# Convolution units that end behind the next eviction, and a light piece behind each convolution piece, in a hybrid decoder trunk

## The chip, the cores and the metric

The kernel runs on one core of one Trainium2 chip. The metric is the time of one execution on the device in microseconds. The core's engines that matter here are PE (TensorE, matrix products), ACT (ScalarE, activations), DVE (VectorE, elementwise work and reductions), POOL (GpSimd) and SP (SyncE, which here only issues loads).

## The reference

Two pre-norm residual layers (`DEPTH` 2) over 256 tokens of width 1024, in float32. Each layer projects the normalised stream once and feeds three causal token mixers side by side; their outputs are projected, gated, merged, projected again and added to the stream. A final RMSNorm closes the trunk. Cut to what matters:

```python
h = rms_norm(x, norm_w[layer])
proj = jnp.einsum('bsd,de->bse', h, w_in[layer])          # 12832 columns
(a_xbc, a_z, a_dt, b_q, b_k, b_v, b_z,
 c_q, c_k, c_v, c_f, c_z, gates) = jnp.split(proj, split_at, axis=-1)
y_a = mamba2_branch(a_xbc, a_z, a_dt, ...)       # convolution of width 4, SiLU, SSD scan, gate, group norm
y_b = sliding_window_branch(b_q, b_k, b_v, b_z, ...)      # rope, window 128, sinks, gate
y_c = forgetting_attention_branch(c_q, c_k, c_v, c_f, c_z, ...)   # decay bias from c_f, gate
branch = jnp.einsum('bsiw,iwd->bsid', jnp.stack([y_a, y_b, y_c], axis=2), w_proj[layer])
g = jax.nn.sigmoid(gates.reshape(b, s, 3, d) + gate_bias[layer])
x = x + jnp.einsum('bsd,de->bse', jnp.sum(g * branch, axis=2), w_out[layer])
```

In the Mamba-2 branch the 2048 columns `a_xbc` (1024 of x, 512 of B, 512 of C) pass a causal depthwise convolution, `silu(sum_j w[j] * u[t-3+j] + bias)`, before the scan.

## The kernel before

**Products.** Every product of activations and weights is made of three float32r products: a value is split into a high part (`hi`) and the remainder (`lo`), and hi x hi, lo x hi and hi x lo are added up in PSUM. A weight part (1024 columns' worth in each of 128 partitions, 512 KB) is loaded by SP into a `raw` tile (six buffers); ACT copies it to `hi` (L261) and DVE subtracts to get `lo` (L262), six buffers each, with at most four parts split ahead (`AHEAD`).

**Pieces and units.** The weights are cut into pieces, mostly of 256 columns (two parts), some of 272 or 512. A piece is worked off in two units. For a 256-column piece of channels (`chan`, L440) a unit is 128 channels by 256 tokens: 24 matmuls into one of three `mm` buffers of PSUM. For token-major pieces (`tok`, L447) a unit is 128 tokens by the piece's columns. Behind its matmuls each unit evicts its PSUM buffer by ACT or DVE and does its own elementwise work:

- convolution (`u_conv`, L672): ACT copies the buffer (L682) and makes bias plus the last tap (L683); DVE adds the other three taps (L686); ACT takes Tanh (L689); DVE closes the SiLU (L690). There are eight such pieces in a layer, 16 units.
- branch gate (`u_z`, L761): ACT Tanh (L770), then DVE (L773, or L777 and L778 for the Mamba branch), which reads the buffer too.
- values of forgetting attention (`u_cv`, L815), its keys (`u_ck`, L833) and queries (`u_cq`, L843): copies on ACT. Two of the value pieces also carry the logits of the time step and of the forget gate.
- merge gate (`u_gate`, L886): DVE adds the bias (L894), ACT takes Tanh (L895).
- projection of a branch (`u_proj`, L900): DVE multiplies by the gate (L936, L939).

**Order.** The order of PE is written out: the list `ops` holds the units, and the loop at L1061 fills it. Before the loop's main part come values, keys and queries of the sliding-window attention. Then, in this stage (the "convolution stage"), B and C of the scan (four convolution pieces) and x (four), with other pieces between them (`lights`, one list for each layer); the swa gate pieces (`zb`), two value pieces (`cv(512, 0)`, `cv(768, 1)`), the merge gates and projection of branch 1 (`gates_proj(1)`). Behind it follow keys, queries and gates of forgetting attention, then branch 0 and branch 2. ACT, DVE and POOL are ordered by the scheduler of the language, which goes by the order of the program and by its own times of what is ready; each engine then runs its list in order.

**The planner.** The work of attention and scan is not in `ops`. It stands in generators that are launched (`launch`, L103) with a branch number and a due time, and are stepped by `pump` (L130) at the end of each unit, when the planner's own clock (an estimate of PE time, L91) has passed the due time and a condition holds. Four quads of heads of sliding-window attention (`swa_quad`, branch 1) follow one another by one token `pp`; each scan group (`ssd_group`, branch 0) waits until no generator of branch 1 is left (L697) and for the token `ssd`; the four quads of forgetting attention (`fox_quad`, branch 2) take the token `bias`, fetch their bias by DMA, wait `D_BDMA` 4.0, mask it on POOL, wait until their queries are there and `D_BIAS` 2.0 more, and then take `pp`. `drain(br)` (L140) forces what is left of a branch. `split_late` (L958) drains a branch and splits its gated output for the projection; in layer 0 it stands a convolution piece ahead of the projection of branch 1, in layer 1 straight ahead of it (L1093, L1134). `group_norm` (L788) is launched with `D_GN1` 4.0 and goes on `D_GN2` 6.0 later.

**Buffers.** Keys and queries of forgetting attention share the four buffers `qt` with the queries of the swa quads. Convolution units use three of the 14 buffers `L1`.

Of the kernel before, what the change touches and what calls it, by code (L numbers as in the profile page):

```python
# [13 lines left out]
AF = mybir.ActivationFunctionType  # L14
ALU = mybir.AluOpType

P = 128
# [6 lines left out]

D_SOFT, D_SOFT2, D_EVAC, D_SSD, D_SSD2 = 7.0, 3.0, 3.0, 8.0, 3.0
D_K, D_Q, D_QK, D_G0, D_FOX, D_BDMA, D_BIAS = 6.0, 5.5, 2.0, 8.0, 0.0, 4.0, 2.0
D_GN1, D_GN2, D_CUM, D_H, D_M = 4.0, 6.0, 12.0, (4.8, 6.4), 5.0
BUDGET = 1.35
T_PP, T_SSD, T_BIAS = 1, 1, 1
N_RAW, N_SPLIT = 6, 6  # L30
# [14 lines left out]
def hybrid_trunk(  # L45
# [17 lines left out]
    def T(tag, shape, dtype=F32, bufs=None):  # L63
        count[0] += 1
        return sb.tile(shape, dtype, tag=tag, name=f"{tag}_{count[0]}",
                       bufs=bufs if bufs is not None else BUFS.get(tag, 1))
# [184 lines left out]
    def halves(ap):  # L251

        return ap.rearrange("p (a i) -> p a i", a=2)
# [418 lines left out]
    def u_conv(y, u, c):  # L672
        def f(w):
            p = chan(y, w, c)
            if u == 8:
                y.bcT = T("L8", [P, 8, S])
            if u == 0:
                y.xs = T("L8", [P, 8, S])
            dst = y.xs[:, u, :] if u < 8 else y.bcT[:, u - 8, :]
            a = T("L1", [P, S])  # L680
            x_ = T("L1", [P, S])
            act(halves(x_), p, AF.Copy)  # L682
            act(halves(a), p, AF.Identity, scale=y.vec[:, 48 + u:49 + u], bias=y.vec[:, 64 + u:65 + u])  # L683
            for j in (2, 1, 0):
                s = 3 - j
                stt(a[:, s:S], x_[:, 0:S - s], y.vec[:, 16 * j + u:16 * j + u + 1], a[:, s:S],  # L686
                    op0=ALU.mult, op1=ALU.add)
            th = T("L1", [P, S])
            act(th, a, AF.Tanh)  # L689
            stt(dst, th, 1.0, a, op0=ALU.add, op1=ALU.mult)  # L690
            if u < 8 and u % 2 == 1:
                launch(0, ssd_group(y, u // 2), D_G0)
            pump()
        return f

    def ssd_group(y, g):
        yield lambda: not any(m[2] == 1 for m in waiting)  # L697
# [63 lines left out]
    def u_z(y, br, u, c):  # L761
        def f(w):
            p = chan(y, w, c)
            if u == 0 and br != 0:
                y.sz[br] = T("L8", [P, NK, S])
            if u == 0 and br == 0:
                y.yh[br] = T("L8", [P, 2, NK, P], F32R)
                y.yl[br] = T("L8", [P, 2, NK, P], F32R)
            th = T("L1", [P, S])
            act(halves(th), p, AF.Tanh, scale=0.5)  # L770
            y.zdone.add((br, u))
            if br != 0:
                stt(halves(y.sz[br][:, u, :]), halves(th), 1.0, p, op0=ALU.add, op1=ALU.mult)  # L773
            else:
                drain(0)
                sz = T("L1", [P, S])
                stt(halves(sz), halves(th), 1.0, p, op0=ALU.add, op1=ALU.mult)  # L777
                tt(y.xs[:, u, :], y.xs[:, u, :], sz, op=ALU.mult)  # L778
                sq = T("L1", [P, S])
                act(sq, y.xs[:, u, :], AF.Square)  # L780
                y.sq.append(sq)
                if u % 2 == 1:
                    tt(y.sq[-2], y.sq[-2], y.sq[-1], op=ALU.add)
                    launch(3 if u < 4 else 4, group_norm(y, u // 2, y.sq[-2]), D_GN1)
            pump()
        return f
# [28 lines left out]
    def u_cv(y, c, t, i=None):  # L815

        def f(w):
            p = tok(y.hTh, y.hTl, w, t)
            if y.cv is None:
                y.cv = T("L8", [P, 2, D])  # L820
            m = w.n if i is None else w.n - 16
            rn = 1.0 if y.rn is None else y.rn[:, t:t + 1]
            if i is None:
                act(halves(y.cv[:, t, c:c + m]), p, AF.Copy, scale=rn)
            else:
                n = w.n // 2
                act(y.cv[:, t, c:c + n], p[:, 0, :], AF.Copy, scale=rn)
                act(y.cv[:, t, c + n:c + m], p[:, 1, 0:m - n], AF.Copy, scale=rn)
                logits(y, t, i, p[:, 1, m - n:n])
            pump()  # L830
        return f

    def u_ck(y, j, c):  # L833
        def f(w):
            p = chan(y, w, c)
            y.ckT[j] = T("qt", [P, 2, S])
            act(halves(y.ckT[j][:, 0, :]), p, AF.Copy)
            if j % 2 == 0:
                launch(2, fox_quad(y, j), D_FOX)
            pump()  # L840
        return f
# [8 lines left out]
        return f  # L850

    def fox_quad(y, j):
        yield "bias"
        bs = []
        for p in range(2):
            bias = T("bias", [P, 2, 3 * P])
            nc.scalar.dma_start(bias[:, :, P:3 * P],
                                y.cumd[2 * (j + p):2 * (j + p) + 2, 1, :].partition_broadcast(P))
            bs.append(bias)
        yield D_BDMA  # L860
        for bias in bs:
            for dst, src in ((slice(0, P), slice(P, 2 * P)), (slice(2 * P, 3 * P), slice(2 * P, 3 * P))):
                for i in range(2):
                    nc.gpsimd.affine_select(out=bias[:, i, dst], in_=bias[:, i, src],  # L864
                                            compare_op=ALU.is_ge, fill=NEG, base=0,
                                            pattern=[[-1, P]], channel_multiplier=1)
        yield lambda: j + 1 in y.cqdone and clock["t"] >= y.cqdone[j + 1] + D_BIAS
        kqs = [y.ckT[j], y.ckT[j + 1]]

        def products(score):  # L870
            for p, kq in enumerate(kqs):
                for b in range(2):
                    for i in range(2):
                        r = slice(64 * i, 64 * i + 64)
                        mm(score(p, i, b), kq[r, 1, b * P:(b + 1) * P], kq[r, 0, 0:(b + 1) * P],
                           start=True, stop=True)

        def scored():
            tokens["bias"] += 1

        yield from attn_quad(products, lambda p, i, b: bs[p][:, i, P * b:P + 2 * P * b], None, y.cv,
                             lambda p, i: slice(P * (j + p) + 64 * i, P * (j + p) + 64 * i + 64),
                             lambda: y.sz[2][:, j:j + 2, :], lambda: (2, j + 1) in y.zdone, scored)


    def u_gate(y, br, c, t):  # L886

        def f(w):
            if t == 0:
                y.gb = T("L2", [P, 512])  # L890
                nc.scalar.dma_start(y.gb, gate_bias[y.l, br:br + 1, c:c + 512].to_broadcast([P, 512]))
            p = tok(y.hTh, y.hTl, w, t)
            g = T("L2", [P, 512])
            tt(halves(g), p, halves(y.gb), op=ALU.add)  # L894
            act(g, g, AF.Tanh, scale=0.5)  # L895
            y.gate[t] = g
            pump()
        return f
# [162 lines left out]
    for y in layers:  # L1061
# [3 lines left out]
        y.gate, y.qT, y.ckT, y.sz, y.yh, y.yl, y.sq, y.h, y.ss, y.var, y.zdone, y.cqdone = {}, {}, {}, {}, {}, {}, [], {}, {}, {}, set(), {}  # L1065
        y.u = y.cv = None
        y.logits = 0

        def cols(c0, n=256):
            return sub([(0, w[:, c0:c0 + n])], n)  # L1070
# [15 lines left out]
        def gates_proj(br):  # L1086
# [3 lines left out]

            def p(b):
                c = 512 * b
                if b == 0 and br != 0 and (br, l) != (1, 0):  # L1093
                    op(None, lambda y=y: split_late(y, br))
                i = sub([(0, w_proj[l, br, :, c:c + 512])], 512)
                if b == 0 and br == 0:
                    op(i, u_proj2(y, br))
                else:
                    op(i, u_proj(y, br, c, 0), u_proj(y, br, c, 1))
# [24 lines left out]
            op(rcols(C_BQ + 256 * g), *u_bq(y, g))  # L1124
        op(None, lambda y=y: layer_vec(y))
        z1(C_ZB, 1, 0)

        cv(512, 0)
        cv(768, 1)
        heavy = [(C_B + 256 * b, 8 + 2 * b) for b in range(4)] + [(C_XS + 256 * b, 2 * b) for b in range(4)]  # L1130
        gp = gates_proj(1)
        zb = [lambda b=b: z1(C_ZB, 1, b) for b in (1, 2, 3)]
        if l == 0:
            lights = {0: [zb[0]], 1: [zb[1]], 3: [zb[2]], 5: [gp.pop(0)], 6: [lambda: op(None, lambda y=y: split_late(y, 1))], 7: [gp.pop(0)]}  # L1134
        else:
            lights = {0: [zb[0]], 2: [zb[1]], 3: [zb[2]], 4: [gp.pop(0)], 6: [gp.pop(0)]}
        for i, (c0, u) in enumerate(heavy):
            op(cols(c0), u_conv(y, u, 0), u_conv(y, u + 1, P))
            for light in lights.get(i, ()):
                light()  # L1140
        for f in gp:
            f()

        for b, zb in enumerate(((), (0,), (1,), (2, 3))):
            op(cols(C_CK + 256 * b), u_ck(y, 2 * b, 0), u_ck(y, 2 * b + 1, P))
            op(cols(C_CQ + 256 * b), u_cq(y, 2 * b, 0), u_cq(y, 2 * b + 1, P))
            for z in zb:
                z1(C_ZC, 2, z)
        for f in gates_proj(0):
# [213 lines left out]
```

## Time and profile before

| | |
|---|---|
| median of 3 runs | 845.81 us (844.84 to 847.25) |
| profiled execution | 846.9 us |
| its span, first to last instruction | 845.2 us |
| PE busy | 828.2 us, 98% |
| DVE busy | 652.4 us, 77% |
| ACT busy | 507.1 us, 60% |
| mean granted clock of PE | 0.996 |

Times in the rows are microseconds from the span's start, and mean times of one instruction are nanoseconds. A row of the timeline gives start, length, engine, line, operation, tiles and shapes; in square brackets stands how long the engine had been idle before it and what it waited for. `hi`, `lo`, `raw`, `mm` (PSUM of the pieces) and `mx` (PSUM of everything else) are tiles; `L` stands for the general SBUF buffers. PE's busy time is modelled, and it is no measure of how full the array is: two matmuls overlap in it.

### The profile page before, as it was taken

The numbers are of one execution on the slowest core, as the hardware profiler recorded it, in microseconds if no ns is written. First come the engines' busy times: TensorE is split into PE (matmuls) and PEld (weight loads), VectorE is DVE, ScalarE is ACT, GpSimd is POOL, SyncE is SP. The second block draws the span as 40 slices with busy tenths as digits, with TensorE's granted clock in tenths as the row PEclk, the third lists the DMA queues.
The fourth block names the chain that finished last, engine by engine and source line by source line (L and its number), as shares of the span: only waits on it lengthen the run. The fifth ranks groups of instructions, "written<-read, shape, count | busy, mean of one in ns | idle before, by whom it ended". The sixth has DMA issues, their size and how long they took to land.

```text
span 845.2 us, 16836 instructions
## 1 busy us (share of the span) xinstructions
PE 828.2 (98%) x6341; PEld 766.2 (91%) x6341; DVE 652.4 (77%) x1418; ACT 507.1 (60%) x1030; POOL 94.2 (11%) x149
## 2 busy tenths in 40 slices
PE   8999999999999999999999999998999999999996
PEld 7999988889999998888999999887899999988896
DVE  6978798898786778665778797988877767785665
ACT  7747667656666666353664676765556666654442
POOL 3330000000111011110005100000001110111000
PEclk9999999999999999999999999999999999999999
DMA  9967554577646556675687556645765565576632
GB/s 302 272 177 223 158 150 146 186 237 202 201 141 180 151 164 215 197 248 177 219 271 207 177 169 214 185 139 187 218 184 163 162 175 151 162 236 212 212 100 75
DMA packets 129563, 159.46 MB, mean 189 GB/s; under 512 B 7970, under 2 KB 98202, under 8 KB 129482
## 3 DMA queue, kind: packets, MB, share of 16 engines
q1 hardware_dynamic: 114960, 140.53, 55.1%
q10 hardware_dynamic: 13690, 16.24, 6.2%
q0 software_dynamic: 832, 1.62, 0.7%
q8 instruction: 50, 0.82, 0.4%
q14 instruction: 31, 0.25, 0.1%
HBM read 154.63 MB, written 2.16 MB: 186 GB/s over the span
## 4 chain that ended last, share of the span: by engine, by line
PE 72%; DVE 14%; ACT 6%; issue 3%; DMA 3%; POOL 0%; SPq 0%; ACTq 0%; POOLq 0%; DVEq 0%
PE mm L97 63%; PE mx L97 6%; DVE lo L262 5%; DVE L L686 3%; PE mx L101 2%; ACT hi L261 2%; DMA L<-cumd 2%; ACT pp L548 2%; DMA L<-in_x_dram 1%; DVE pp L560 1%; DVE L L690 1%; DVE L L262 1%; ACT L L577 1%; DVE pp L542 1%; DVE L L724 1%
## 5 line engine op out<-in xcount | busy, mean ns | idle before, releaser
L262 DVE TENSOR_TENSOR lo<-raw,hi 128x1024 fp32r<-128x1024 f32 (+2 forms) x276 | 315.6, 1159 | 85.1 <-ACT hi L261 78.7
L97 PE MATMUL mm<-L,hi 128*128 128x256 f32 x2112 | 373.2, 278 | 3.3 <-ACT L L683 1.6
L97 PEld LDWEIGHTS mm<-L,hi 128*128 128x128 f32 x2112 | 326.9, 192 | 11.8 <-issue 6.0
L261 ACT ACTIVATE hi<-raw 128x1024 fp32r<-128x1024 f32 (+2 forms) x276 | 266.3, 981 | 104.8 <-PE mm L97 85.5
L97 PE MATMUL mm<-hi,L 128*128 128x512 f32 (+2 forms) x1232 | 325.1, 352 | 3.0 <-DVE L L262 2.7
L97 PE MATMUL mm<-L,lo 128*128 128x256 f32 x1056 | 290.4, 275 | 0.0
L97 PEld LDWEIGHTS mm<-hi,L 128*128 128x128 f32 x1232 | 217.5, 190 | 27.3 <-DVE L L262 3.5
L97 PE MATMUL mm<-lo,L 128*128 128x512 f32 (+2 forms) x616 | 214.2, 349 | 0.0
L97 PEld LDWEIGHTS mm<-L,lo 128*128 128x128 f32 x1056 | 202.6, 192 | 0.1
L97 PEld LDWEIGHTS mm<-lo,L 128*128 128x128 f32 x616 | 116.7, 190 | 11.7
L864 POOL TENSOR_SCALAR_AFFINE_SELECT bias<-bias 128x128 f32<-128x128 f32 x64 | 29.5, 498 | 398.9 <-DMA bias<-cumd 381.5
L548 ACT ACTIVATE pp<-pp,nm 128x128 f32<-128x128 f32 (+1 forms) x128 | 56.6, 443 | 16.3 <-DVE nm L542 16.1
L686 DVE SCALAR_TENSOR_TENSOR L<-L,vec,L 128x255 f32<-128x255 f32 (+2 forms) x96 | 45.9, 478 | 2.0 <-ACT L L683 0.9
L689 ACT ACTIVATE L<-L 128x256 f32<-128x256 f32 x32 | 13.4, 417 | 46.5 <-DVE L L686 46.5
L560 DVE TENSOR_SCALAR pp<-pp,rsum 128x128 f32<-128x128 f32 (+1 forms) x128 | 32.2, 315 | 0.5
L770 ACT ACTIVATE L<-mm 128x256 f32<-128x256 f32 x48 | 17.9, 372 | 22.2 <-PE mm L97 18.1
L895 ACT ACTIVATE L<-L 128x512 f32<-128x512 f32 x24 | 15.1, 628 | 25.8 <-DVE L L894 25.5
L577 ACT ACTIVATE L<-mx 128x512 f32<-128x512 f32 x48 | 27.0, 595 | 1.8 <-PE mx L101 1.4
L101 PE MATMUL mx<-ident,pp 128*128 128x128 f32 x192 | 26.8, 275 | 0.0
L542 DVE CUSTOM_DVE_ANT_0 pp<-mx,wmask,nsink 128x128 f32<-128x128 f32 x64 | 23.9, 411 | 1.4 <-PE mx L97 1.4
L261 ACT ACTIVATE L<-L 128x512 fp32r<-128x512 f32 (+1 forms) x36 | 18.4, 531 | 10.8 <-DVE L L811 7.3
L894 DVE TENSOR_TENSOR L<-mm,L 128x512 f32<-128x512 f32 x24 | 16.4, 684 | 9.9 <-PE mm L97 9.9
(190 smaller groups left out, 719.5 us busy)
## 6 DMA issues: line engine op xcount, KB each, us to landing
raw<-in_w_in_dram SPq DMA_DIRECT2D x191, 512.0 KB, 4.6
raw<-in_w_proj_dram SPq DMA_DIRECT2D x48, 512.0 KB, 4.8
raw<-in_w_out_dram SPq DMA_DIRECT2D x16, 512.0 KB, 4.9
L<-cumd ACTq DMA_DIRECT2D x8, 512.0 KB, 6.2
bias<-cumd ACTq DMA_DIRECT2D x16, 256.0 KB, 4.0
L<-in_gate_bias_dram ACTq DMA_DIRECT2D x12, 256.0 KB, 5.3
raw<-in_w_in_dram SPq DMA_DIRECT2D x4, 408.0 KB, 3.5
raw<-in_w_in_dram SPq DMA_DIRECT2D x4, 384.0 KB, 4.9
```

The costliest lines, as they stand in the source:

```text
L97: nc.tensor.matmul(o, a, b, **kw)
L101: nc.tensor.transpose(o, a, i)
L261: keep(act)(hi, src, AF.Copy)
L262: keep(tt)(lo, src, hi.bitcast(F32), op=ALU.subtract)
L542: nc.vector.tensor_tensor_reduce(out=pp[:, i, sl], in0=score(p, i, b), in1=biases(p, i, b), scale=-0.125, scalar=1.0e30 if ns is None else ...
L548: act(pp[:, i, sl], pp[:, i, sl], AF.Exp, scale=-1.0, bias=nm[:, e:e + 1], accum_out=sums[:, e:e + 1])
L560: ts(pp[:, i, sl], pp[:, i, sl], rs[:, 2 * i + b:2 * i + b + 1], 0.5, op0=ALU.mult, op1=ALU.mult)
L577: act(pT, pt, AF.Copy)
L686: stt(a[:, s:S], x_[:, 0:S - s], y.vec[:, 16 * j + u:16 * j + u + 1], a[:, s:S], op0=ALU.mult, op1=ALU.add)
L770: act(halves(th), p, AF.Tanh, scale=0.5)
L864: nc.gpsimd.affine_select(out=bias[:, i, dst], in_=bias[:, i, src], compare_op=ALU.is_ge, fill=NEG, base=0, pattern=[[-1, P]], channel_mul ...
L894: tt(halves(g), p, halves(y.gb), op=ALU.add)
```

## The change

A convolution unit is cut in two. Its eviction and its three taps stay; Tanh, the closing multiply and the launch of the scan group become a function `end`, which is put on a list. The next unit that calls `finish` behind its own eviction on ACT runs what is on the list, with its ACT instructions queued behind that eviction (`issue_after` fixes the order on ACT, without a wait). Convolution, gate, value, key and merge-gate units call it; queries and projections do not.

The two layers now have one order. Two swa gate pieces come first, and then each of the eight convolution pieces is followed by one other piece: the two value pieces, two swa gate pieces, the first merge gate of branch 1, the first keys and the first queries of forgetting attention, and the first projection of branch 1 with `split_late` straight ahead of it, in both layers. The quads of forgetting attention wait for a flag, `y.fox`, which is set behind the projection of branch 1. `D_GN1` goes from 4.0 to 5.0.

```diff
-D_GN1, D_GN2, D_CUM, D_H, D_M = 4.0, 6.0, 12.0, (4.8, 6.4), 5.0
+D_GN1, D_GN2, D_CUM, D_H, D_M = 5.0, 6.0, 12.0, (4.8, 6.4), 5.0
...
-            act(halves(a), p, AF.Identity, scale=y.vec[:, 48 + u:49 + u], bias=y.vec[:, 64 + u:65 + u])
+            finish(act(halves(a), p, AF.Identity, scale=y.vec[:, 48 + u:49 + u], bias=y.vec[:, 64 + u:65 + u]))
             for j in (2, 1, 0):
                 s = 3 - j
                 stt(a[:, s:S], x_[:, 0:S - s], y.vec[:, 16 * j + u:16 * j + u + 1], a[:, s:S],
                     op0=ALU.mult, op1=ALU.add)
-            th = T("L1", [P, S])
-            act(th, a, AF.Tanh)
-            stt(dst, th, 1.0, a, op0=ALU.add, op1=ALU.mult)
-            if u < 8 and u % 2 == 1:
-                launch(0, ssd_group(y, u // 2), D_G0)
+            def end():
+                th = T("L1", [P, S])
+                act(th, a, AF.Tanh)
+                stt(dst, th, 1.0, a, op0=ALU.add, op1=ALU.mult)
+                if u < 8 and u % 2 == 1:
+                    launch(0, ssd_group(y, u // 2), D_G0)
+            ends_later.append(end)
             pump()
         return f
+    ends_later = []
+    def finish(out):
+        with tc.issue_after(out.ins):
+            while ends_later:
+                ends_later.pop(0)()
...
     def fox_quad(y, j):
+        yield lambda: y.fox
         yield "bias"
...
-                if b == 0 and br != 0 and (br, l) != (1, 0):
+                if b == 0 and br != 0:
                     op(None, lambda y=y: split_late(y, br))
...
         z1(C_ZB, 1, 0)
-        cv(512, 0)
-        cv(768, 1)
+        z1(C_ZB, 1, 1)
         heavy = [(C_B + 256 * b, 8 + 2 * b) for b in range(4)] + [(C_XS + 256 * b, 2 * b) for b in range(4)]
         gp = gates_proj(1)
-        zb = [lambda b=b: z1(C_ZB, 1, b) for b in (1, 2, 3)]
-        if l == 0:
-            lights = {0: [zb[0]], 1: [zb[1]], 3: [zb[2]], 5: [gp.pop(0)], 6: [lambda: op(None, lambda y=y: split_late(y, 1))], 7: [gp.pop(0)]}
-        else:
-            lights = {0: [zb[0]], 2: [zb[1]], 3: [zb[2]], 4: [gp.pop(0)], 6: [gp.pop(0)]}
+        lights = [lambda: cv(512, 0), lambda: cv(768, 1), lambda: z1(C_ZB, 1, 2), lambda: z1(C_ZB, 1, 3),
+                  gp.pop(0), lambda: ck(0), lambda: cq(0), gp.pop(0)]
         for i, (c0, u) in enumerate(heavy):
             op(cols(c0), u_conv(y, u, 0), u_conv(y, u + 1, P))
-            for light in lights.get(i, ()):
-                light()
+            lights[i]()
         for f in gp:
             f()
-        for b, zb in enumerate(((), (0,), (1,), (2, 3))):
-            op(cols(C_CK + 256 * b), u_ck(y, 2 * b, 0), u_ck(y, 2 * b + 1, P))
-            op(cols(C_CQ + 256 * b), u_cq(y, 2 * b, 0), u_cq(y, 2 * b + 1, P))
+        op(None, lambda y=y: setattr(y, "fox", True))
+        for b, zb in ((1, (0,)), (2, (1,)), (3, (2, 3))):
+            ck(b)
+            cq(b)
             for z in zb:
                 z1(C_ZC, 2, z)
```

`ck(b)` and `cq(b)` add the key and the query piece b, as the two removed lines did.

More of the change, by code (lines that the diff above doesn't have):

```diff
@@ L769, in f @@
             th = T("L1", [P, S])
-            act(halves(th), p, AF.Tanh, scale=0.5)
+            finish(act(halves(th), p, AF.Tanh, scale=0.5))
             y.zdone.add((br, u))
@@ L823, in f @@
             if i is None:
-                act(halves(y.cv[:, t, c:c + m]), p, AF.Copy, scale=rn)
+                finish(act(halves(y.cv[:, t, c:c + m]), p, AF.Copy, scale=rn))
             else:
@@ L827, in f @@
                 act(y.cv[:, t, c:c + n], p[:, 0, :], AF.Copy, scale=rn)
-                act(y.cv[:, t, c + n:c + m], p[:, 1, 0:m - n], AF.Copy, scale=rn)
+                finish(act(y.cv[:, t, c + n:c + m], p[:, 1, 0:m - n], AF.Copy, scale=rn))
                 logits(y, t, i, p[:, 1, m - n:n])
@@ L836, in f @@
             y.ckT[j] = T("qt", [P, 2, S])
-            act(halves(y.ckT[j][:, 0, :]), p, AF.Copy)
+            finish(act(halves(y.ckT[j][:, 0, :]), p, AF.Copy))
             if j % 2 == 0:
@@ L894, in f @@
             tt(halves(g), p, halves(y.gb), op=ALU.add)
-            act(g, g, AF.Tanh, scale=0.5)
+            finish(act(g, g, AF.Tanh, scale=0.5))
             y.gate[t] = g
@@ L1067, in hybrid_trunk @@
         y.logits = 0
+        y.fox = False
         def cols(c0, n=256):
@@ L1126, in hybrid_trunk, with ck, cq @@
         z1(C_ZB, 1, 0)
-        cv(512, 0)
-        cv(768, 1)
+        z1(C_ZB, 1, 1)
         heavy = [(C_B + 256 * b, 8 + 2 * b) for b in range(4)] + [(C_XS + 256 * b, 2 * b) for b in range(4)]
         gp = gates_proj(1)
-        zb = [lambda b=b: z1(C_ZB, 1, b) for b in (1, 2, 3)]
-        if l == 0:
-            lights = {0: [zb[0]], 1: [zb[1]], 3: [zb[2]], 5: [gp.pop(0)], 6: [lambda: op(None, lambda y=y: split_late(y, 1))], 7: [gp.pop(0)]}
-        else:
-            lights = {0: [zb[0]], 2: [zb[1]], 3: [zb[2]], 4: [gp.pop(0)], 6: [gp.pop(0)]}
+        def ck(b):
+            op(cols(C_CK + 256 * b), u_ck(y, 2 * b, 0), u_ck(y, 2 * b + 1, P))
+        def cq(b):
+            op(cols(C_CQ + 256 * b), u_cq(y, 2 * b, 0), u_cq(y, 2 * b + 1, P))
+        lights = [lambda: cv(512, 0), lambda: cv(768, 1), lambda: z1(C_ZB, 1, 2), lambda: z1(C_ZB, 1, 3),
+                  gp.pop(0), lambda: ck(0), lambda: cq(0), gp.pop(0)]
         for i, (c0, u) in enumerate(heavy):
             op(cols(c0), u_conv(y, u, 0), u_conv(y, u + 1, P))
-            for light in lights.get(i, ()):
-                light()
+            lights[i]()
         for f in gp:
             f()
-        for b, zb in enumerate(((), (0,), (1,), (2, 3))):
-            op(cols(C_CK + 256 * b), u_ck(y, 2 * b, 0), u_ck(y, 2 * b + 1, P))
-            op(cols(C_CQ + 256 * b), u_cq(y, 2 * b, 0), u_cq(y, 2 * b + 1, P))
+        op(None, lambda y=y: setattr(y, "fox", True))
+        for b, zb in ((1, (0,)), (2, (1,)), (3, (2, 3))):
+            ck(b)
+            cq(b)
             for z in zb:
```

## The prediction, on record before the result was known

> **What bounds the kernel now.** I read the page first, then busy time by stretch, then the PE's own waits, then what stood ahead of the instruction that ended each wait. The page, and the stretches (columns: length, PE, weight loads, DVE, ACT, POOL, clock, DMA share, GB/s):
>
> ```profile
> span 845.2 us, 16836 instructions
> ...
> PE 828.2 (98%) x6341; PEld 766.2 (91%) x6341; DVE 652.4 (77%) x1418; ACT 507.1 (60%) x1030; POOL 94.2 (11%) x149
> ...
> raw<-in_w_in_dram SPq DMA_DIRECT2D x191, 512.0 KB, 4.6
> ```
> ```profile
> 54.00:182.00 128.00, 125.11 (x1080) 115.57 (x1079) 110.14 (x290) 87.75 (x210) 5.97 (x14) 1.00 0.58 176
> 182.00:416.00 234.00, 233.71 (x1661) 214.53 (x1661) 170.17 (x338) 133.40 (x248) 25.18 (x33) 1.00 0.63 192
> 288.00:324.00 36.00, 35.71 (x290) 33.89 (x287) 27.34 (x63) 23.91 (x47) 4.35 (x4) 1.00 0.53 155
> 468.00:585.00 117.00, 113.32 (x977) 104.76 (x977) 99.72 (x271) 80.40 (x199) 5.64 (x14) 0.99 0.57 176
> ```
>
> PE is the bound, and the change neither adds nor removes a matmul. What can be won is what PE loses waiting: 2.9 us in the convolution stage of layer 0 (54 to 182), 3.7 us in that of layer 1 (468 to 585), 0.3 us in the long stretch behind. There DVE is busy for 86% (110.14 of 128), against 73% in the long stretch. These are its larger waits there, by the timeline:
>
> ```profile
> 119.31 0.28 PE L97 MATMUL mm<-L,hi 128*128 128x256 f32 x1
> 121.19 0.38 PE L97 MATMUL mm<-L,hi 128*128 128x256 f32 x1 [1.61 <-ACT L L683]
> ...
> 128.19 0.38 PE L97 MATMUL mm<-L,hi 128*128 128x256 f32 x1 [0.72 <-DVE L L773]
> ...
> 539.70 0.38 PE L97 MATMUL mm<-L,hi 128*128 128x256 f32 x1 [0.51 <-DVE L L773]
> ...
> 563.75 0.35 PE L97 MATMUL mm<-L,hi 128*128 128x256 f32 x1 [0.46 <-DVE L L894]
> ...
> 575.00 0.38 PE L97 MATMUL mm<-lo,L 128*128 128x512 f32 x1
> 575.22 0.38 PE L97 MATMUL mm<-hi,L 128*128 128x512 f32 x1
> 578.31 0.80 PE L97 MATMUL mm<-hi,L 128*128 128x512 f32 x1 [2.71 <-DVE L L262]
> 578.89 0.63 PE L97 MATMUL mm<-lo,L 128*128 128x512 f32 x1
> 579.32 1.06 PE L97 MATMUL mm<-hi,L 128*128 128x512 f32 x2
> 580.17 0.63 PE L97 MATMUL mm<-lo,L 128*128 128x512 f32 x1
> 580.60 1.06 PE L97 MATMUL mm<-hi,L 128*128 128x512 f32 x2
> 581.46 0.47 PE L97 MATMUL mm<-lo,L 128*128 128x512 f32 x1
> 581.76 0.60 PE L97 MATMUL mm<-hi,L 128*128 128x512 f32 x2
> ```
>
> The first four stand where a new unit needs a PSUM buffer (there are three `mm` buffers) that has not been evicted. ACT around the first two, DVE for the second, and ACT for the third:
>
> ```profile
> 119.99 0.42 ACT L689 ACTIVATE L<-L 128x256 f32<-128x256 f32 x1 [1.84 <-DVE L L686]
> 120.32 0.37 ACT L682 ACTIVATE L<-mm 128x256 f32<-128x256 f32 x1
> 120.58 0.56 ACT L683 ACTIVATE L<-mm,vec 128x256 f32<-128x256 f32 x1
> ...
> 126.93 0.42 ACT L689 ACTIVATE L<-L 128x256 f32<-128x256 f32 x1 [2.38 <-DVE L L686]
> ```
> ```profile
> 127.73 0.41 DVE L773 SCALAR_TENSOR_TENSOR L<-L,mm 128x256 f32<-128x256 f32 x1
> ```
> ```profile
> 538.22 0.42 ACT L689 ACTIVATE L<-L 128x256 f32<-128x256 f32 x1 [0.60 <-DVE L L686]
> ```
>
> The Tanh that closes a convolution unit (L689) stands on ACT ahead of the next unit's eviction (L682 and L683 of a convolution, or the Tanh of a gate with DVE's L773 behind it), and waits there for the unit's three multiply-adds on a full DVE. PE's buffer is free only after that.
>
> **The change, part by part.** Durations that I use (columns: count, busy us, mean ns, idle before), and, from the chain of waits, a 256-column piece on PE, two units of 24 matmuls:
>
> ```profile
> L262 DVE TENSOR_TENSOR lo<-raw,hi 128x1024 fp32r<-128x1024 f32 (+2 forms) x276 | 315.6, 1159 | 85.1 <-ACT hi L261 78.7 <-PE mm L97 4.9
> ...
> L686 DVE SCALAR_TENSOR_TENSOR L<-L,vec,L 128x255 f32<-128x255 f32 (+2 forms) x96 | 45.9, 478 | 2.0 <-ACT L L683 0.9
> ...
> L690 DVE SCALAR_TENSOR_TENSOR L<-L,L 128x256 f32<-128x256 f32 x32 | 13.5, 421 | 6.5 <-ACT L L689 6.5
> ...
> L689 ACT ACTIVATE L<-L 128x256 f32<-128x256 f32 x32 | 13.4, 417 | 46.5 <-DVE L L686 46.5
> ```
> ```profile
> 271.38 5.36 PE mm L97 x48
> ```
>
> *Ends behind the next eviction.* 32 Tanh and 32 closing multiplies move; none is added, so their own cost is nil. ACT waits 46.5 us ahead of Tanh in all, but only the waits that reach PE are worth time: the first is 121.19 − 119.31 = 1.88, less the usual 0.11 (5.36/48), so 1.77; that is its idle time plus 0.16, and so the others are 0.88 and 0.67. Sum 3.3 us. Tanh stood idle 1.84, 2.38 and 0.60 us there. With a unit more of grace (2.68 us) all three waits would go, since each is shorter: **−3.3**. The least is 0, if ACT only waits a unit later. Tanh now comes 2.7 us later, or behind a whole 10 us projection piece for the last unit; what reads it, a scan group, is launched from the same place with 8 planner microseconds to spare.
>
> *A light piece behind each convolution piece.* A convolution piece costs DVE 2 × 1.159 + 6 × 0.478 + 2 × 0.421 = 6.0 us, more than PE's 5.36; a key or query piece of forgetting attention costs it only the two splits, 2.3 us. Two convolution pieces in a row (two such pairs ahead of the projection in each layer) put 12.1 us of DVE under 10.7 us of PE; after, none stand together. The moved pieces (two of forgetting attention ahead of the projection; the two value pieces, one swa gate piece and, in layer 0, the merge-gate piece by a few places) bring all their work with them: the same matmuls, splits, evictions and loads on the SP queue, in another order. The load queue keeps six parts ahead, 16 us of PE, against a landing of 4.6 us, so loads cost nothing; without that lead each moved part would cost up to that. DVE's total up to the projection grows by 4.6 us in 10.7 us of PE, so its share stays near 86%, and I keep a small new wait in each layer, priced by the 0.51 row plus 0.16: **+1.3** (from 0 to twice that).
>
> *The projection behind the last convolution piece.* The large wait is for the last part of the gated swa output in `split_late`:
>
> ```profile
> 571.84 0.68 DVE L590 TENSOR_TENSOR L<-mx,L 128x512 f32<-128x512 f32 x1
> ...
> 577.58 0.68 DVE L262 TENSOR_TENSOR L<-L,L 128x512 fp32r<-128x512 f32 x1
> ```
>
> From L590 to the end of that split pass 6.4 us, and PE asked for it at 575.44, 3.6 us after L590 began. The swa quads keep their place in PE's order, while the projection comes two pieces, 10.7 us, later, less the 0.67 of waits gone ahead of it: 13.6 us of room against 6.4. The wait goes: 578.31 − 575.22 − 0.22 = 2.87. Behind it eight matmuls take 581.76 − 578.31 = 3.45 us in place of 8 × 0.22, at half rate: 1.69 more. **−4.6.** Layer 0 loses the convolution piece that stood between its splits and its projection, but has the same room.
> The Trainium skill, TensorE: Matmul & The Clock Gate, section What's actually happening, gives about 3.4 us of idleness as what halves the clock; here 2.71 us were enough, so the trace and the page differ. By the page the 1.69 us would not belong to this wait and the sum would be 1.7 us smaller.
>
> *The merge-gate piece* (two 512-column units) is followed by a convolution piece in layer 1 already, where the 0.46 us wait for L894 stands: splits, not Tanh, are ahead of it. That order now comes in layer 0 too: **+0.6** (0 to 1.2).
>
> *Forgetting attention's gate.* Its first quad no longer starts at its keys but when the flag is set behind the projection, then takes 4.0 planner microseconds, so two units. Rows of the first and last scores, the last quad's DVE work, and, below, what the stage behind leaves free:
>
> ```profile
> 216.53 1.58 PE L97 MATMUL mx<-qt 64*128 64x128 f32 x16
> ...
> 282.68 1.58 PE L97 MATMUL mx<-qt 64*128 64x128 f32 x16
> ```
> ```profile
> 283.75 0.29 DVE L542 CUSTOM_DVE_ANT_0 pp<-mx,bias 128x128 f32<-128x128 f32 x1
> ...
> 287.94 1.01 DVE L560 TENSOR_SCALAR pp<-pp,rsum 128x128 f32<-128x128 f32 x4
> ...
> 320.91 0.42 DVE L262 TENSOR_TENSOR L<-L,L 128x256 fp32r<-128x256 f32 x1
> ```
> ```profile
> 324.40 5.18 PE mm L97 x24
> ```
>
> The quads follow one another by one token, so the last slides by two units, 5.4 us, into the stretch 288 to 324, where DVE has 36 − 27.3 = 8.7 us free and its work is 288.95 − 283.75 = 5.2. I cost it at **0**; the cover is that free time. D_GN1 one higher moves a step of the norm by at most one unit: 0, or 0.3 us in each layer either way.
>
> The sum: −3.3 − 4.6 + 1.3 + 0.6 = **−6.0 us**. The profiled execution took 846.9 us (1.7 around its span); it would be 840.9. The median of the runs is 845.81, 1.1 below, so 839.8.
>
> **The rivals.**
> *A, DVE is the bound and Tanh blocks one unit later.* For it: 86% stays 86%, and ACT runs in order (L682 at 120.32 starts as soon as L689 lets it). Against: the pairs are gone. The 3.3 us stay, the large wait goes: −4.6 + 1.3 + 0.6 = −2.7, so 843.1. The same page, section Architectural detail, calls ScalarE and VectorE strict first-in first-out, which speaks for this rival and agrees with the order of the rows.
> *B, the last quad of forgetting attention delays the norm.* The part that the projection at 324.40 needs is ready at 321.3, 3.1 us early. If all 5.2 us come ahead of it, PE waits 2.1 + 0.2 in each layer: −6.0 + 4.6 = −1.4, so 844.4. Against: the 8.7 us.
> *C, the other side: `split_late` is late in both layers.* It now stands straight ahead of the projection in layer 0 too, and DVE has the first scan group to do there, as in layer 1 where the split at 577.58 waited behind it. Then layer 1 keeps its 4.6 and layer 0 gains one: −3.3 + 4.6 + 1.3 + 0.6 = +3.2, so 849.0. It decides where the swa product comes less than 6.4 us ahead of PE's need, that is, if the quads slip by over 6 us against the pieces. Nothing in the planner's rules moves them so.
>
> **How the numbers follow.** Forecast 0.60, A 0.16, B 0.12, C 0.12. A measurement tells 0.3%, 2.5 us, from no change: 843.3 and 848.3 are the bounds. A lies on the first, so half of it counts as faster with some 0.01 more: faster 0.69, the same 0.19, slower 0.12. The forecast's own range is 836.5 (all waits and the 0.6 of the norm gone, no new ones) to 842. For 8 in 10 I take in A and B with the bound of the new waits: 836.5 to 846.5; C stays out.
>
> **What would show it.** Right: in both stages no PE wait put down to L683 or L773 over 0.7 us; ACT's idle time ahead of L689 well under 46.5 us; no PE wait for L262 at the branch 1 projection in either layer, and clock 1.00 there. Wrong: waits as before a unit further on (A); PE waits or a fallen clock at the first projection of branch 0 (B); 2 to 3 us ahead of the branch 1 projection (C). The forecast fails if PE's idle time in the two stages together stays above 4 us.

## The result, and the profile after

The changed kernel takes 837.44 us (median of four runs, 837.33 to 838.13) against 845.45 us of the kernel before (four runs, 844.84 to 847.25) on the same chip: a ratio of 0.9903, with a 95% interval from 0.9886 to 0.9921, or 8.0 us less. The forecast was 839.8 us.

The profiled execution took 837.55 us. From the page, its span and the busy times of the engines:

```profile
span 835.8 us, 16820 instructions
...
PE 825.6 (99%) x6341; PEld 766.2 (92%) x6341; DVE 651.9 (78%) x1418; ACT 509.3 (61%) x1030; POOL 114.4 (14%) x149
```

The matmuls are the same 6341 and DVE has the same work. Of the 9.4 us by which the span is shorter, 6.8 are idle time of PE (17.0 us before, 10.2 now) and 2.6 are modelled busy time, most of that the matmuls at half rate. Busy time by stretch (length, PE, weight loads, DVE, ACT, POOL, clock, DMA share, GB/s): the convolution stage of layer 0, the stretch behind it, the part of that in which the norm runs, and the convolution stage of layer 1:

```profile
54.00:190.00 136.00, 136.00 (x1185) 127.83 (x1184) 121.51 (x310) 94.94 (x223) 11.58 (x14) 1.00 0.60 185
190.00:410.00 220.00, 219.12 (x1540) 199.98 (x1540) 157.57 (x315) 126.03 (x233) 29.36 (x33) 1.00 0.60 186
280.00:316.00 36.00, 35.84 (x304) 33.45 (x302) 27.42 (x76) 24.61 (x57) 3.29 (x3) 1.00 0.44 140
462.00:593.00 131.00, 131.00 (x1168) 123.53 (x1167) 116.12 (x305) 92.86 (x220) 12.17 (x15) 1.00 0.58 181
```

PE is busy throughout both convolution stages, where it lost 2.9 and 3.7 us before, and the clock is 1.00 in both. DVE is fuller than before: 121.51 of 136 us is 89%, 116.12 of 131 is also 89%, against 86% and 85%. The stretch behind, which lost 0.3 us in 234 before, now loses 0.9 in 220. All waits of PE that the view shows in the whole run after, summed by what ended them (us in total, times, longest):

```profile
PE mx L101 <- POOL ident masks.py:199: 1.5, 1, 1.5
PE mx L97 <- ACT L L815: 1.4, 2, 0.7
PE mm L97 <- DVE L L262: 0.4, 2, 0.2
```

The same view of the kernel before, with its larger rows and the one for the merge gate:

```profile
PE mm L97 <- DVE L L262: 2.7, 1, 2.7
PE mm L97 <- ACT L L683: 1.6, 1, 1.6
PE mx L101 <- POOL ident masks.py:199: 1.5, 1, 1.5
PE mm L97 <- DVE L L773: 1.2, 2, 0.7
PE mx L97 <- DVE L L783: 0.6, 2, 0.3
...
PE mm L97 <- DVE L L894: 0.5, 1, 0.5
...
```

The wait for `ident` is the start of the kernel and stands in both. All waits for evictions and for `split_late` are gone. The two that are new lie at the end of the norm and in the first projection of branch 0, once in each layer (L815, line 804 before, makes the matrix by which the norm's scale is spread):

```profile
316.53 0.78 PE L97 MATMUL mx<-L,ones 128*128 128x128 f32 x4 [0.69 <-ACT L L815]
...
329.82 0.48 PE L97 MATMUL mm<-hi,L 128*128 128x512 f32 x1 [0.18 <-DVE L L262]
```

In the groups by line, ACT's idle time ahead of the Tanh that closes a convolution (now L690) has fallen from 46.5 us to 12.2:

```profile
L690 ACT ACTIVATE L<-L 128x256 f32<-128x256 f32 x32 | 13.2, 413 | 12.2 <-DVE L L686 9.6 <-DVE dt L645 2.6
```

### The profile page after: what moved, and what is told of

Same layout as the page of the kernel before. It is cut to its first block, busy times and chain, and to the rows that moved or that the text cites. A ratio compares the mean times of both kernels' runs of the same rounds, so it can differ in the third digit from the quotient of the medians.

```text
span 835.8 us, 16820 instructions
## 1 busy us (share of the span) xinstructions
PE 825.6 (99%) x6341; PEld 766.2 (92%) x6341; DVE 651.9 (78%) x1418; ACT 509.3 (61%) x1030; POOL 114.4 (14%) x149
## 4 chain that ended last, share of the span: by engine, by line
PE 52%; DVE 5%; ACT 1%; issue 1%; POOL 1%; DMA 1%; POOLq 0%; ACTq 0%; DVEq 0%
PE mm L97 47%; PE mx L97 4%; DVE lo L262 2%; PE mx L101 2%; DMA L<-in_x_dram 1%; DVE L L262 1%; ACT hi L261 1%; POOL sm L807 1%; DVE L L788 0%; ACT L L815 0%; DVE L L789 0%; DVE L L822 0%; DVE pp L542 0%; DVE L L906 0%; DVE pp L560 0%
## 5 line engine op out<-in xcount | busy, mean ns | idle before, releaser
L262 DVE TENSOR_TENSOR lo<-raw,hi 128x1024 fp32r<-128x1024 f32 (+2 forms) x276 | 314.4, 1156 | 77.5 <-ACT hi L261 70.2
L97 PE MATMUL mm<-L,hi 128*128 128x256 f32 x2112 | 371.4, 278 | 0.0
L97 PEld LDWEIGHTS mm<-L,hi 128*128 128x128 f32 x2112 | 326.0, 192 | 7.8 <-issue 6.4
L97 PE MATMUL mm<-hi,L 128*128 128x512 f32 (+2 forms) x1232 | 324.3, 351 | 0.7 <-DVE L L262 0.4
L97 PE MATMUL mm<-L,lo 128*128 128x256 f32 x1056 | 290.4, 275 | 0.0
L97 PEld LDWEIGHTS mm<-hi,L 128*128 128x128 f32 x1232 | 217.2, 190 | 25.2 <-DVE L L262 1.6
L97 PE MATMUL mm<-lo,L 128*128 128x512 f32 (+2 forms) x616 | 213.6, 348 | 0.0
L97 PEld LDWEIGHTS mm<-L,lo 128*128 128x128 f32 x1056 | 202.7, 192 | 0.0
L97 PEld LDWEIGHTS mm<-lo,L 128*128 128x128 f32 x616 | 116.3, 190 | 11.5
L876 POOL TENSOR_SCALAR_AFFINE_SELECT bias<-bias 128x128 f32<-128x128 f32 x64 | 46.5, 766 | 383.2 <-DMA bias<-cumd 293.4
L781 ACT ACTIVATE L<-mm 128x256 f32<-128x256 f32 x48 | 18.0, 374 | 19.2 <-PE mm L97 19.2
L952 POOL TENSOR_TENSOR L<-L,L 128x512 f32<-128x512 f32 x8 | 15.9, 1998 | 59.6 <-DVE L L951 45.0
```

Source lines behind the costliest of these rows:

```text
L97: nc.tensor.matmul(o, a, b, **kw)
L262: keep(tt)(lo, src, hi.bitcast(F32), op=ALU.subtract)
L781: finish(act(halves(th), p, AF.Tanh, scale=0.5))
```

## The experiments

The theory is that of the prediction. The rivals stand in each expectation. Times are medians, and the ratio is that to the kernel before on the same chip, which took 846.3 us beside the first group of runs (`e1` to `e5`), 846.28 beside the second (`e6` to `e9`) and 847.08 beside the third. Line numbers are those of the changed kernel; where the order of the kernel before stands in a variant, the parts behind that order move by a few lines.

### One part alone

**The deferred ends without the order** (`e1`): the kernel before, with this and the calls of `finish` alone; its own order, `D_GN1` 4.0, no flag.

```diff
-            th = T("L1", [P, S])
-            act(th, a, AF.Tanh)
...
+            def end():
+                th = T("L1", [P, S])
+                act(th, a, AF.Tanh)
...
+            ends_later.append(end)
```

> The order of pieces, the due times and the start of forgetting attention are those of before; only the ends of the convolution units are put behind the next eviction. Theory (the forecast's terms add up): the waits of PE for L683 and for L773 go, 3.3 us, the wait of 2.7 us for the split ahead of the projection of layer 1 and its slow clock stay, 4.6 us, and so does the 0.6 for L894: 845.4 - 3.3 = 842.1. Rival A (DVE is the bound, Tanh blocks one unit later): evictions still wait, 845 or above.

Measured: 841.03 us, ratio 0.9941 (0.9919 to 0.9964), 5.3 us faster. The largest waits of PE beside the start's, and the row of the first of them:

```profile
PE mm L97 <- DVE L L262: 2.0, 1, 2.0
...
PE mm L97 <- DVE L L784: 1.2, 1, 1.2
PE mx L97 <- DVE L L753: 1.1, 2, 0.7
PE mm L97 <- ACT L L683: 0.8, 1, 0.8
```
```profile
575.51 0.48 PE L97 MATMUL mm<-hi,L 128*128 128x512 f32 x1 [1.96 <-DVE L L262]
```

The time is near the theory's, but not for its reason. Deferring the ends did not clear the waits at evictions: 1.2 us (L784, the multiply of a gate unit) and 0.8 us (L683) of them are left. The first stands at the same unit as the wait of 0.72 us before. The rows ahead of it show why the deferred Tanh did not help there: ACT had done the gate's own Tanh (L781) by 124.00, but on DVE a split, a closing multiply and the last tap came before the multiply that frees the buffer.

```profile
123.64 0.36 ACT L781 ACTIVATE L<-mm 128x256 f32<-128x256 f32 x1
```
```profile
124.05 1.22 DVE L262 TENSOR_TENSOR lo<-raw,hi 128x1024 fp32r<-128x1024 f32 x1
...
125.53 0.48 DVE L686 SCALAR_TENSOR_TENSOR L<-L,vec,L 128x253 f32<-128x253 f32 x1
125.92 0.41 DVE L784 SCALAR_TENSOR_TENSOR L<-L,mm 128x256 f32<-128x256 f32 x1
```

The wait for `split_late` is there as in the kernel before, 1.96 us in place of 2.71, and the matmuls behind it run at full speed: 0.75 us and the 1.69 of half rate are saved there. With 3.3 − 2.0 at the evictions (the waits of the view, 1.6 + 1.2 + 0.5 before) that is 3.7 us; 1.1 us of waits at products of the scan (L753) came on top, against 0.2 before, so that the rows account for 2.8 of the 5.3 us.

**The order without the deferred ends** (`e2`, and again as `e7` beside other runs):

```diff
-            ends_later.append(end)
+            end()
```

> The new order with all its due times, but each convolution unit ends at once, as before. Theory: the wait of 2.7 us ahead of the projection and its slow clock go, 4.6 us; of the 3.3 us of late evictions at least half stay, because Tanh is ahead of the next eviction again while DVE is busy for 86%: 839 to 841. Rival (the order alone does it, since no two convolution pieces stand together): no wait for an eviction, 837.5.

Measured: 840.44 us, ratio 0.9932 (0.9919 to 0.9945). Waits of PE, and the group of the Tanh:

```profile
PE mx L97 <- ACT L L815: 1.4, 2, 0.7
PE mx L97 <- DVE L L753: 1.0, 3, 0.4
PE mm L97 <- DVE L L262: 0.4, 2, 0.2
```
```profile
L690 ACT ACTIVATE L<-L 128x256 f32<-128x256 f32 x32 | 13.3, 417 | 40.1 <-DVE L L686 33.9 <-DVE dt L645 4.2 <-DVE u L615 2.0
```

ACT stands ahead of the Tanh for 40.1 us, nearly as long as before, and still no eviction reaches PE: the order alone removes every wait for L683 and for the gates' multiply, and that for `split_late` too. What is left of the ends shows as three waits at products of the scan for L753.

> The new order with convolution units that end at once, again, now beside the changed kernel. Theory after the first runs (without pairs the deferred ends are worth only what the profile of that order shows, some 1.0 us of waits at the scan's products for L753): 0.5 to 1.5 us above the changed kernel. Rival (the ends are worth what the first runs on different chips suggest): 2.5 to 3.5 us above it.

Measured: 841.26 us, ratio 0.9941 (0.9927 to 0.9955). **The changed kernel** ran beside it:

> The changed kernel again, beside the next ones on the same chip. Both theories: 7.5 to 8.5 us below the kernel before, about 838.

Measured: 837.52 us, ratio 0.9898 (0.9884 to 0.9912). So the deferred ends are worth 841.26 − 837.52 = 3.7 us on top of the order, more than the theory and the rival gave. The two convolution stages of the order alone:

```profile
54.00:190.00 136.00, 135.44 (x1179) 126.49 (x1178) 120.44 (x309) 94.84 (x223) 5.98 (x14) 1.00 0.60 182
462.00:593.00 131.00, 130.39 (x1167) 122.09 (x1166) 113.73 (x298) 90.10 (x217) 13.63 (x16) 1.00 0.60 178
```

PE is idle for 0.56 + 0.61 = 1.2 us there, none of it in the changed kernel. The other 2.5 us are no waits of the view. Measured from one matmul's start to the next's, PE spends 12.92 us in place of 11.69 on the small products of the scan (its waits there included), 19.23 in place of 18.44 on the transposes of probabilities, and 12.55 in place of 11.61 on the products of the quads with their values: 3.0 us in all, the most of it in pieces too short to be told as waits.

**First keys and queries of forgetting attention put back behind the projection** (`e5`): the rest of the change stays.

```diff
-                  gp.pop(0), lambda: ck(0), lambda: cq(0), gp.pop(0)]
+                  gp.pop(0), lambda: None, lambda: None, gp.pop(0)]
...
-        for b, zb in ((1, (0,)), (2, (1,)), (3, (2, 3))):
+        for b, zb in enumerate(((), (0,), (1,), (2, 3))):
```

> The changed kernel, but the first keys and queries of forgetting attention stand behind the projection again, so that the last three convolution pieces stand together and the projection comes 10.7 us earlier. Theory (room of the swa product): in layer 1 of the changed kernel the product L590 comes at 562.9 and its split is done at 572.0, while the projection asks for it at about 588; 10.7 us earlier, 577, is still behind 572, so no wait for the split; three convolution pieces give DVE 18.1 us under 16.1 of PE, so up to 2 us of new waits: 837.4 to 839.5. Rival (these pieces are what covers the splits): the wait and the slow clock come back in one layer or both, 842 or more.

Measured: 842.79 us, ratio 0.9958 (0.9941 to 0.9975), about 5 us slower than the changed kernel. Waits of PE:

```profile
PE mx L97 <- DVE L L753: 3.6, 4, 1.2
PE mx L97 <- DVE sm L810: 1.7, 2, 0.8
...
PE mm L97 <- ACT L L683: 0.2, 1, 0.2
```

What came are 3.6 us at products of the scan, which wait for DVE's L753, and 1.7 us at the norm, where the changed kernel has 1.4. The waits at evictions did not come back but for 0.2 us, and the view shows none for `split_late`; yet that one was near. Its rows in layer 1, on DVE and on PE:

```profile
566.55 0.69 DVE L590 TENSOR_TENSOR L<-mx,L 128x512 f32<-128x512 f32 x1
...
578.22 0.68 DVE L262 TENSOR_TENSOR L<-L,L 128x512 fp32r<-128x512 f32 x1
```
```profile
574.50 0.68 PE L97 MATMUL mm<-hi,L 128*128 128x512 f32 x2
...
578.47 0.98 PE L97 MATMUL mm<-hi,L 128*128 128x512 f32 x2
```

The split ends at 578.90, just in the pair of matmuls that takes 0.98 us in place of its usual 0.59: it is some 0.4 us late. Without the two light pieces the room is used up to the last; the larger cost, though, is the waits at the first scan groups. That DVE lacks the time there which these pieces gave it fits the rows, and was not tried apart.

### The norm's step and the flag

**`D_GN1` back to 4.0** (`e3`), everything else changed:

```diff
-D_GN1, D_GN2, D_CUM, D_H, D_M = 5.0, 6.0, 12.0, (4.8, 6.4), 5.0
+D_GN1, D_GN2, D_CUM, D_H, D_M = 4.0, 6.0, 12.0, (4.8, 6.4), 5.0
```

> The changed kernel with D_GN1 back at 4.0. The changed kernel has one new wait of PE in each layer, 0.7 us for L815 (the norm's diagonal) at the first projection of branch 0, and 0.2 us for a split there. Theory 1 (the later due time makes it): both go, 836.0. Theory 2 (rival B in small: the last quad of forgetting attention is later): they stay, 837.4, or the older 0.3 us waits for the sum of squares come on top, 838.

Measured: 842.06 us, ratio 0.9951 (0.9937 to 0.9964): 4.6 us slower than the changed kernel by the medians, 4.1 to 4.5 by the ratios, since the two ran on different chips; every theory had expected none or a small difference. The wait, and its row in layer 1:

```profile
PE mx L97 <- DVE L L794: 4.4, 2, 2.2
```
```profile
718.69 0.61 PE L97 MATMUL mx<-ones,L 128*128 128x2 f32 x4 [2.17 <-DVE L L794]
```

The sum of squares of the norm stands in PE's order one unit too early: PE reaches it before DVE has added the squares (L794), and everything behind it on PE waits for 2.2 us, in each layer. Against the changed kernel's 1.8 us (L815 and L262, which are gone here) that is 2.6 more, and in layer 1 the clock falls behind the wait (last section), some 1.7 us by estimate.

**`D_GN1` 5.0 in the kernel before** (`e8`):

```diff
-D_GN1, D_GN2, D_CUM, D_H, D_M = 4.0, 6.0, 12.0, (4.8, 6.4), 5.0
+D_GN1, D_GN2, D_CUM, D_H, D_M = 5.0, 6.0, 12.0, (4.8, 6.4), 5.0
```

> The kernel before with D_GN1 5.0 in place of 4.0 and nothing else. Theory (the later due time is a cure for what the new order brings, where 4.0 costs 2.2 us a layer): in the old order it is worth at most the two waits of 0.3 us, so 0 to 0.6 us below the kernel before. Rival (4.0 is too early in any order): 4 us below it.

Measured: 847.43 us, ratio 1.0009 (0.9996 to 1.0021). In the old order it is worth nothing that can be measured; the wait for `split_late` stands there as ever (`PE mm L97 <- DVE L L262`, 3.1 us in all, 2.7 of them there). So 5.0 mends something that the new order makes.

**The flag ahead of the projection of branch 1, `D_GN1` 4.0** (`e9`), which is three pieces earlier, the two halves of the projection and the merge gate between them:

```diff
+            if i == 7:
+                op(None, lambda y=y: setattr(y, "fox", True))
             lights[i]()
...
-        op(None, lambda y=y: setattr(y, "fox", True))
```

> The changed kernel with D_GN1 4.0 and with the flag of forgetting attention set ahead of the projection of branch 1 instead of behind it, so that the quads start three or four 10 us units earlier. Theory (rival B of the forecast: the quads' slide into the gates of branch 0 is what makes 4.0 too early): the wait of PE for L794, 2.2 us a layer with 4.0, falls to 0.3 or less: 837 to 838.5. Rival (the slide has no part in it, the norm's step has merely moved over a unit's end): the 2.2 us stay: 842.

Measured: 834.98 us (834.42 to 835.23), ratio 0.9866 (0.9851 to 0.9882): **faster than both kernels**, 11.3 us under the kernel before. These are all waits of PE that the view shows, and its stretch of the norm:

```profile
PE mx L101 <- POOL ident masks.py:199: 1.5, 1, 1.5
PE mx L101 <- DMA L<-in_x_dram: 0.3, 1, 0.3
```
```profile
280.00:316.00 36.00, 36.00 (x309) 34.49 (x305) 27.29 (x64) 23.45 (x45) 3.35 (x3) 1.00 0.54 156
```

Behind the start, no wait of PE is left in the view. The scores of the last quad of forgetting attention, first in the changed kernel and then in this one:

```profile
285.67 1.58 PE L97 MATMUL mx<-qt 64*128 64x128 f32 x16
```
```profile
275.20 1.58 PE L97 MATMUL mx<-qt 64*128 64x128 f32 x16
```

Only the flag lies between this kernel and `e3`, and it is worth 842.06/846.3 against 834.98/846.28 of the kernel before, 0.9951 − 0.9866 = 0.0085, or 7 us. The late quads are what makes `D_GN1` 4.0 too short.

**The flag earlier with `D_GN1` 5.0** (`e10`):

> The changed kernel with the flag of forgetting attention set ahead of the projection of branch 1, D_GN1 5.0 kept: the fourth corner of the square of flag (behind, ahead) and D_GN1 (5.0: 837.5; 4.0: 842.1 behind, 835.0 ahead). Theory (the late quads disturb the norm, and 5.0 only softens it): with the quads out of the way 5.0 is as good as 4.0, 835 to 836. Rival (5.0 itself makes the waits of 0.7 us for L815, whatever the quads do): they stay, 836.5 to 837.5.

Measured: 836.58 us, ratio 0.9876 (0.9857 to 0.9895). The waits for L815 are gone, and three short ones for L262 are left, two of which stand in the changed kernel too:

```profile
PE mm L97 <- DVE L L262: 0.7, 3, 0.2
```

The time lies in the rival's range, while the waits that the rival kept are gone, as the theory has it; against `e9`, the intervals of the ratios overlap, so which value of `D_GN1` is better with the flag ahead stays open.

**`e9` with its ends at once** (`e11`), the edit of `e2`:

> The fastest version so far (flag ahead, D_GN1 4.0, 835.0), but with convolution units that end at once. Theory (the deferred ends are worth some 3.5 us in the new order too, by many small waits at the scan's and the quads' products and not at evictions): 838 to 839. Rival (with the quads moved the ends no longer matter): 835 to 836.

Measured: 839.83 us, ratio 0.9917 (0.99 to 0.9934), 0.005 or 4 us behind `e9`. The products of the scan, in the groups by line, of `e11`:

```profile
L97 PE MATMUL mx<-L,L 128*64 128x128 f32 x192 | 16.8, 278 | 1.1 <-DVE L L753 0.9
```

and of `e9`:

```profile
L97 PE MATMUL mx<-L,L 128*64 128x128 f32 x192 | 16.3, 277 | 0.0
```

Here too the ends are worth about 4 us, no wait at an eviction is among them, and what can be seen is about a microsecond at the scan. From one small product's start to the next matmul's, PE also spends 1.3 us more on the transposes of probabilities (20.13 against 18.83 us in all), 1.2 on the scan's (12.91 against 11.69, its waits included) and 0.6 on those of the quads (12.18 against 11.61): 3.1 of the 3.7 us by which these two profiled executions differ, the most of it in pieces too short to be told as waits.

## Why the prediction was right or wrong

**What bounds the kernel: right.** PE was the bound, the matmuls did not change, and the time came from PE's waits. The median moved by 8.0 us. The profiled executions differ by 9.35, of which 1.45 is that the one of before lay above its median (846.9 against 845.45).

**The sum: right in its two large terms, mis-sized in the small ones.** The eviction waits of 3.3 us and the 4.6 us at the branch 1 projection are gone from the rows, 7.9 together. Two terms went wrong, both upwards. *A light piece behind each convolution piece* carried +1.3 for new waits in the stages, and *the merge-gate piece* +0.6 for waits for its addition; PE's idle time in both stages is 0, so both are 0, although DVE's share rose to 89%. The +0.6 rested on a misreading besides: in the order of before the merge-gate piece is followed by a convolution piece in layer 0 too, without a wait there. The stages also gave up the rest of their old idle time (6.6 us in all, of which the four large waits had 5.6), and the norm's old waits for L783, 0.6. On the other side stand 2 × (0.7 + 0.2) = 1.8 us of new waits that the sum had at nothing. So −7.9 − 1.0 − 0.6 + 1.8 = −7.7, which is near the −8.0 of the medians. The rows are of the profiled executions, though, which differ by 9.35. Most of the rest shows from one matmul's start to the next's: the transposes of probabilities take 18.45 us in place of 19.52 and the small products of the scan 11.69 in place of 12.74. The sum had no term for them.

**The step that says which part brings which term: wrong.** The prediction gave *ends behind next eviction* the 3.3 us and the order the 4.6. The runs show parts that overlap: ends alone 5.3 us, order alone 5.0 to 5.9, both 8.0 to 8.8. "With a unit more of grace all three waits would go" failed in `e1`, where 2.0 us of waits at evictions are left, 1.2 of them behind DVE's own list and not behind a Tanh. The order removes them without the ends: with it, ACT stands 40.1 us ahead of Tanh in `e2` and no eviction is late. What the prediction had not seen is that a deferred Tanh is worth 3.7 us where no eviction waits. About 1 us of that is shown as waits and some 2 more as time of small products of scan and attention. That ACT, free for other work, lets these products wait less for DVE and ACT is argued and was not tried.

**The room for `split_late`: right that the wait goes, wrong in both sizes.** Forecast were 13.6 us from the last swa product to PE's need, against a chain of 6.4. The rows of layer 0 and of layer 1 on DVE, and the projection's first matmuls in layer 0:

```profile
153.17 0.68 DVE L590 TENSOR_TENSOR L<-mx,L 128x512 f32<-128x512 f32 x1
...
161.61 0.68 DVE L262 TENSOR_TENSOR L<-L,L 128x512 fp32r<-128x512 f32 x1
...
562.86 0.68 DVE L590 TENSOR_TENSOR L<-mx,L 128x512 f32<-128x512 f32 x1
...
571.29 0.69 DVE L262 TENSOR_TENSOR L<-L,L 128x512 fp32r<-128x512 f32 x1
```
```profile
174.61 0.68 PE L97 MATMUL mm<-hi,L 128*128 128x512 f32 x2
...
178.58 0.59 PE L97 MATMUL mm<-hi,L 128*128 128x512 f32 x2
```

The chain now takes 9.1 us (153.17 to 162.29), since DVE has other work between. PE starts the projection at 174.61 and comes to the late part with the second matmul of the pair at 178.58, about 178.8: 25.6 us of room. In layer 1 the projection comes three pieces later and not two, 16.1 us in place of 10.7, since in the order of before the last convolution piece stood behind it there. "The swa quads keep their place" was wrong too, for the good: in layer 1 the last product comes at 562.86, 9.0 us earlier than the 571.84 of before, where some 4 us are the time that the kernel had gained by then. In `e5`, with 10.7 us of pieces less and a chain of 12.4 (566.55 to 578.90), nothing was to spare.

**`D_GN1` at "0, or 0.3 us in each layer either way": the step that failed.** In the new order the constant is worth 4 us or more (`e3`), some 2 a layer, about seven times the bound. The prediction weighed it against the old order, where it is indeed worth nothing (`e8`). It belongs to the step ahead of it, the gate of forgetting attention: the sum had the last quad slide by two units; its scores came three units later in PE's order, at 285.67, behind the second unit of the gate piece that stands there, and its transposes fall among the norm's steps, whose due time the planner counts in PE's work. That the flag is the cause is shown (`e9` against `e3`); the way through the planner's clock is argued. Slide and constant were both put at 0, and they nearly offset one another: with the constant left at 4.0 the same order takes 842.06 us. That the forecast held here is luck.

**Rivals.** A, that DVE is the bound, fell with the idle time of 0 in both stages; in the old order, `e1`, one gate unit does wait for DVE. C fell: in the changed kernel the chain has 16 us to spare, and `e5`, the nearest to it, has it late by 0.4 us in one layer. **B had the right place.** The late quads do press on the norm; `D_GN1` 5.0 hides most of it, and 0.9 us a layer in place of B's 2.3 are what is left; with 4.0 the wait is 2.2 us a layer, near B's price, though at the squares and not at the last part that the projection needs. With the flag ahead (`e9`) those are gone too. The prediction had the cover as free time of DVE, 8.7 us against 5.2; the free time was there (36 − 27.42 = 8.6), and yet the norm was late, since what counts is in which unit PE asks for the squares, and not how much DVE has free in the stretch.

## What to carry to other kernels

In an order that is written out by hand, a due time may be right for one order only, as `D_GN1` was here: when the work around it slides, move the due time by hand and alone, and look in the trace for the first matmul that asks one unit too early. A gain that the trace credits to one part can be had from another, so test each part alone and both together before telling which one did it. Follow a slid producer to the place where its reader stands in the queue; free time in the stretch is no cover if the reader's turn comes before it.

## What the runs showed of the hardware

**The clock after a wait.** In `e3` the same wait of 2.2 us stands in both layers of one execution. The windows of 4 us behind it, layer 0 and layer 1 (the clock is the eighth value):

```profile
308.00:312.00 4.00, 4.00 (x39) 3.53 (x39) 2.98 (x13) 3.76 (x9) 1.05 (x1) 1.00 0.49 141
...
719.00:723.00 4.00, 4.00 (x25) 3.03 (x25) 2.98 (x13) 2.90 (x8) 1.05 (x1) 0.57 0.49 137
```

Once the clock stays at 1.00, once it falls to 0.57, with 25 matmuls in place of 39. The wait of 1.96 us in `e1` left it at 1.00 (576 to 580). One of 1.94 us in `e8`, the kernel before with `D_GN1` 5.0, was followed by 0.50 (124.5 to 126.5), and that of 2.71 us before by 0.52 (578.31 to 581.76). So a wait of 2.2 us can cost some 1.7 us more (0.43 of 4 us, an estimate), or nothing, and its length alone does not decide. The Trainium skill, TensorE: Matmul & The Clock Gate, section What's actually happening, gives an idle window of some 3.4 us as what halves the clock; no wait here was so long, and yet the clock fell, so the trace differs from the page. What decides between the two cases was not tried.
